# Column-first queries, values by column group and paired tables in a hybrid neighbourhood-attention and mLSTM layer

## The chip, the core and the metric

The kernel runs on one core of a Trainium2 chip. The metric is the device time of one execution in microseconds (us), and lower is better. The kernel before was run three times: 1325.43, 1327.04 and 1330.51 us, median 1327.04.

## What is computed

One layer over 2048 tokens (a grid of 32 rows by 64 columns) of width 1024. Cut to what matters:

```python
h = rmsnorm(x) * (1 + scale) + shift           # scale, shift, gate from c
proj = h @ w_in + b_in                         # 1024 -> 4624 columns
na_q, na_k, na_v, na_z, ml_q, ml_k, ml_v, ml_o, ml_z, i_f, f_f, i_b, f_b = split(proj)
# neighbourhood attention, 8 heads of 64: each query sees 8 rows x 16 columns of keys
s = (na_q * 64**-0.5) . k_neighbours + bias    # bias from rpb, outside the window -inf
na_out = softmax(s) @ v_neighbours * silu(na_z)
# bidirectional mLSTM, 4 heads of 128, chunks of 64 tokens; here a short conv goes ahead of q, k
mq, mk = silu(conv5(ml_q)), silu(conv5(ml_k))
hm = (mlstm(mq, mk, ml_v, i_f, f_f) + flipped(mlstm(...))) * sigmoid(ml_o)
ml_out = layernorm_per_head(hm) * ml_norm_w * silu(ml_z)
y = concat(na_out, ml_out) @ w_out
out = rmsnorm(x + gate * y) * final_norm_w
```

Everything is float32. A product is made of three TensorE passes over operands split into a high and a low part (`whi`, `wlo`, `hhi`, `hlo`).

## The kernel before

**Stages.** The kernel holds h for all tokens in SBUF (four groups of 512 tokens) and goes over the columns of w_in in blocks.

1. `tok_blocks` makes values token by token, one PSUM tile of 128 tokens x 256 columns after another: four blocks for the mLSTM (`vo_group`, tiles `pvo`), then two blocks, 4 and 5, for the attention values (`nav_group`, tiles `pv`). A tile is 24 matmuls; four tiles make a group of 512 tokens. VectorE adds the bias while it moves each tile into a staging tile `stv` (L581), and after the fourth tile the staging tile is stored to `d_vna` in device memory (L586). The two blocks make eight groups, so eight stores. There are two staging tiles, so group g+2 can be moved only after the store of group g has landed; and there are four PSUM tiles, so TensorE can run four tiles ahead of VectorE. Beside it a chain of small jobs runs: `decays` loads a tile `dec` of 256 KB on the SP queue (L822), POOL and ACT work on it, and the ACT queue stores it to `d_ck`; 32 such tiles go through six buffers. `tables_columns` and `tables_rows` (L670) build the tables of bias and mask in device memory, `d_t`, by copies from `d_e`, also on the SP queue.
2. `conv_blocks` makes the mLSTM's q and k with the short conv.
3. `phase1b` runs the two mLSTM passes, whose small matmuls are interleaved with a stream of large ones from `nq_gen`: the columns of mz, nz, k and q. Those for attention patches and for mz are made in patch order: TensorE writes the tile `pq` (L986), ACT moves it out with its bias (L1015, L1020), and for q and k VectorE makes the low part (L1021). At the end of each chunk of the mLSTM, `turn` transposes hm with a permutation `perm` into patch order (L1282), and `end` multiplies it into `zt` (L1288).
4. `phase2` is the attention and the output projection. A patch is 8 rows x 16 columns = 128 queries, and there are 16 patches; a unit is one patch and one pair of heads, 64 units (54 loads of a pair of tables, since a few units use the tables of an earlier one). `scores` makes the scores of both heads of two units (`pS`, L1477), VectorE adds the table `tab` and takes the minimum (L1485), ACT makes the exponential (L1486), VectorE normalises (L1497), TensorE transposes in `turned` (`pT`, L1505) and multiplies with the values (`pO`, L1520). `load_tab` (L1449) loads a table, on SP's queue, as soon as the reduce that read the same buffer is done; two units' worth of buffers exist, each of two tables. `outproj` makes `y` (L1565), adds it to x and stores the row tile to `out` (L1608, for the last patch L1599 and L1601). `load_x` (L1426), the value loads (L1405) and the stores go through POOL's queue.

**What sets the order.** Each engine works its own instructions in order, and SP's and POOL's DMA issues are such instructions. In the first stages a scheduler fixes the order when the program is built; in phase 2 it is written by hand.

The two staging tiles alternate here, and the store is held back to the middle of the next group:

```python
st = self.stage_tile(f"stv_{blk}_{g}")
for o in range(4):
    ...
    next(self.chain, None)
    if o == 1:
        self.flush()
...
self.defer(lambda: nc.sync.dma_start(dst, st[:, :, :256]))
```

Of the kernel before, what the change touches and what calls it, by code (L numbers as in the profile page):

```python
# [8 lines left out]
F32 = mybir.dt.float32  # L9
F32R = mybir.dt.float32r  # L10
AF = mybir.ActivationFunctionType
# [4 lines left out]
P = 128  # L16
# [34 lines left out]
def patch_order(ap):  # L51
    return ap.rearrange("p (r a k) -> p a r k", a=4, k=16)


def patch_ps(ap):
    return ap.rearrange("p (a r k) -> p r a k", a=4, k=16)
# [6 lines left out]
class Kernel:  # L63
# [30 lines left out]
    def scratch(self):  # L94
        d = self.dram
        self.d_vna = d.tile([T, 512], F32, name="d_vna")
# [4 lines left out]
        self.d_qna = d.tile([2, 2, 16, P, 2, P], F32, name="d_qna")  # L101
# [9 lines left out]
        self.d_t = [[d.tile([NH, P, nrs[r] * nks[t]], F32, name=f"d_t{r}{t}") for t in range(3)] for r in range(3)]  # L111
# [462 lines left out]
    def nav_group(self, blk, slot, g):  # L574
# [10 lines left out]
        dst = self.d_vna[g * GT : (g + 1) * GT, c0 : c0 + 256].rearrange("(o p) c -> p o c", p=P)  # L585
        self.defer(lambda: nc.sync.dma_start(dst, st[:, :, :256]))  # L586
# [53 lines left out]
    def tables_columns(self, ct):  # L640
# [3 lines left out]
        for i in range(16):  # L644
            c = c0 + i
            start = min(max(c - 8, 0), GRID_W - 16)
            dx = start - c + 15
            nc.sync.dma_start(self.d_e[ct][:, i, :, start - k0 : start - k0 + 16], self.d_rneg[:, :, dx : dx + 16])

    def table_fills(self):  # L650
        nc = self.nc
        for ct in range(3):
            for rt in range(3):
                t = self.d_t[rt][ct]
                n = t.shape[-1]
                dst = t.rearrange("h q k -> (h q k)").rearrange("(p j k) -> p j k", p=P, j=16)
# [3 lines left out]
    def tables_rows(self, ct, rt):  # L660
# [4 lines left out]
        for r in range(8):  # L665
# [5 lines left out]
                t[:, r * 16 : (r + 1) * 16, j0 : j0 + 8 * nk],  # L671
                self.d_e[ct][:, :, dy : dy + 8, :].rearrange("h c a k -> h c (a k)"),
# [292 lines left out]
    def nq_gen(self):  # L965
# [10 lines left out]
        for i, s, g in order:  # L976
# [35 lines left out]
            hv, lv = both[:, 0:512], both[:, 512:1024]  # L1012
            if kind in ("mz", "nz"):
                hv = hv.bitcast(F32)
                nc.scalar.activation(hv, ps, AF.Silu, bias=bias)  # L1015
# [3 lines left out]
            else:  # L1019
                nc.scalar.activation(hv, ps, AF.Identity, bias=bias)  # L1020
                nc.vector.scalar_tensor_tensor(lv, ps, bias, hv.bitcast(F32), ALU.add, ALU.subtract)  # L1021
                for e, part in enumerate((hv, lv)):
                    src = part.bitcast(F32).rearrange("p (a q) -> p a q", a=4)
                    if kind == "q":
                        dst = self.d_qna[e, ct // 2, 4 * g : 4 * g + 4, :, ct % 2].rearrange("a p q -> p a q")
# [23 lines left out]
    def phase1b(self, left, right):  # L1049
# [11 lines left out]
        self.perm = self.mle.tile([P, P], F32, name="perm")  # L1061
        nc.vector.tensor_copy(self.perm.rearrange("p (a r k) -> p a r k", r=2, k=16), patch_order(self.ident))
# [125 lines left out]
    def ml_pass2(self, ml, h):  # L1188
# [88 lines left out]
        def turn(c):  # L1277
# [4 lines left out]
            nc.tensor.transpose(ps, hm[gi][:, o, :], self.perm)  # L1282
# [533 lines left out]
```

## Time and profile before

| what | value |
|---|---|
| median of three runs | 1327.04 us |
| profiled execution, its span (the page gives no other time of it) | 1326.9 us |
| TensorE matmuls (PE) busy | 1294.6 us, 98% of the span |
| VectorE (DVE) busy | 779.6 us, 59% |
| ScalarE (ACT) busy | 542.8 us, 41% |
| GpSimd (POOL) busy | 225.1 us, 17% |
| moved by DMA | 255.91 MB, mean 193 GB/s |

The stages in time: the start and the mLSTM's values up to about 236 us, the attention's values from 236 to 329 us, the conv to about 520, the mLSTM passes with the stream of columns to about 950, the attention and output after that. A row of the views names the line, the engine, the operation and what it writes and reads; "waits" are the idle time of an engine and what ended it; PEld is TensorE's weight load, which runs beside PE; SPq, ACTq and POOLq are the queues that issue DMAs.

### The profile page before, as it was taken

What the parts mean: (1) busy time and instruction counts of PE and PEld (TensorE: products, weight loads), DVE (VectorE), ACT (ScalarE), POOL (GpSimd) and SP (SyncE); (2) the same over time, 40 slices, a digit from 0 to 9 for tenths busy, and PEclk for the clock granted to TensorE, in tenths of its full rate; (3) what the DMA queues carried; (4) which work ended last, traced back from release to release, by engine and by line L of the source; (5) the groups of instructions that cost most, each with busy time, mean ns of one, the idle gap of its engine ahead of it and who ended that gap; (6) DMA issues with size and microseconds to landing.
All of it is one profiled execution on the core that took longest, in us unless ns stands there. A gap on an engine that the chain in (4) does not pass through costs nothing. (4 is left out here: it accounts for less than half of the span.)

```text
span 1326.9 us, 23404 instructions
## 1 busy us (share of the span) xinstructions
PE 1294.6 (98%) x8330; PEld 1115.4 (84%) x8330; DVE 779.6 (59%) x2406; ACT 542.8 (41%) x1184; POOL 225.1 (17%) x280
## 2 busy tenths in 40 slices
PE   9999999999999999999999999999999999999996
PEld 8899999999878787888888888888777778778785
DVE  5754452112455559176768878767547576666663
ACT  5643324543222323123324323333356555565551
POOL 0243103331000000012212002121202211212211
PEclk9999999999999999999999999999999999999999
DMA  9998657998267685545756866746689977868871
GB/s 325 323 281 180 169 141 171 214 244 217 82 149 208 142 209 165 159 120 167 204 165 196 254 187 204 237 141 188 198 256 239 212 184 190 195 175 194 195 186 48
DMA packets 240487, 255.91 MB, mean 193 GB/s; under 512 B 31079, under 2 KB 200295, under 8 KB 240371
## 3 DMA queue, kind: packets, MB, share of 16 engines
q1 hardware_dynamic: 157006, 182.98, 50.7%
q0 software_dynamic: 20496, 36.21, 11.2%
q10 hardware_dynamic: 62868, 35.22, 9.6%
q8 instruction: 66, 1.08, 0.4%
q14 instruction: 51, 0.41, 0.1%
HBM read 169.81 MB, written 92.72 MB: 198 GB/s over the span
## 5 line engine op out<-in xcount | busy, mean ns | idle before, releaser
L986 PE MATMUL pq<-hhi,whi_a 128*128 128x512 f32 x512 | 208.2, 407 | 0.8 <-ACT u L891 0.8
L986 PE MATMUL pq<-hlo,whi_a 128*128 128x512 f32 x512 | 208.4, 407 | 0.0
L986 PE MATMUL pq<-hhi,wlo_a 128*128 128x512 f32 x512 | 206.7, 404 | 0.0
L986 PEld LDWEIGHTS pq<-hhi,whi_a 128*128 128x128 f32 x512 | 96.8, 189 | 17.8 <-ACT u L891 1.3
L986 PEld LDWEIGHTS pq<-hhi,wlo_a 128*128 128x128 f32 x512 | 96.8, 189 | 16.3
L986 PEld LDWEIGHTS pq<-hlo,whi_a 128*128 128x128 f32 x512 | 96.7, 189 | 16.0 <-issue 0.5
L1507 ACT ACTIVATE pt<-pT 96x384 f32<-96x384 f32 (+3 forms) x128 | 65.8, 514 | 86.7 <-PE pT L1505 84.0
L1486 ACT ACTIVATE pbuf<-pbuf,mn 128x480 f32<-128x480 f32 (+5 forms) x128 | 76.0, 594 | 53.0 <-DVE mn L1485 53.0
L960 POOL TENSOR_TENSOR wlo_a<-rawq,whi_a 128x1024 fp32r<-128x1024 f32 x19 | 45.8, 2409 | 296.1 <-ACT whi_a L959 263.7
L1565 PE MATMUL y<-hhi,whi_a 128*128 128x512 f32 x256 | 91.4, 419 | 0.5 <-ACT whi_a L1535 0.5
L1565 PE MATMUL y<-hhi,wlo_a 128*128 128x512 f32 (+1 forms) x272 | 90.7, 399 | 0.2 <-ACT y L1572 0.2
L1485 DVE CUSTOM_DVE_ANT_0 pbuf<-pS,tab 128x480 f32<-128x480 f32 (+5 forms) x128 | 62.9, 540 | 39.1 <-PE pS L1477 32.1
L1230 ACT ACTIVATE num<-px,gtile 128x129 f32<-128x129 f32 x120 | 38.3, 366 | 111.3 <-PE px L1225 86.5
L1505 PEld LDWEIGHTS pT<-ident,pbuf 128*128 128x128 f32 (+2 forms) x416 | 51.0, 137 | 29.6 <-issue 9.9
L618 DVE TENSOR_TENSOR stvo<-pvo,brow 128x256 f32<-128x256 f32 x64 | 26.6, 422 | 83.1 <-PE pvo L548 65.7
L1505 PE MATMUL pT<-ident,pbuf 128*128 128x128 f32 (+2 forms) x416 | 67.3, 275 | 8.2 <-DVE pbuf L1497 6.8
L546 PE MATMUL pvo<-whi_b,hhi 128*128 128x256 f32 x256 | 72.6, 284 | 0.0
L548 PE MATMUL pvo<-whi_b,hlo 128*128 128x256 f32 x256 | 72.1, 281 | 0.0
L547 PE MATMUL pvo<-wlo_b,hhi 128*128 128x256 f32 x256 | 72.0, 281 | 0.0
L1249 POOL TENSOR_TENSOR hm<-hm,ck 128x128 f32<-128x128 f32 x64 | 26.5, 414 | 252.9 <-DVE hm L1248 223.9
L833 ACT ACTIVATE dec<-dec,gtile 128x128 f32<-128x128 f32 x128 | 42.7, 393 | 53.6 <-POOL dec L826 50.8
L581 DVE TENSOR_TENSOR stv<-pv,brow 128x256 f32<-128x256 f32 x32 | 12.4, 421 | 74.4 <-DMA d_vna<-stv 43.4
(302 smaller groups left out, 3408.3 us busy)
## 6 DMA issues: line engine op xcount, KB each, us to landing
ck<-d_ck SPq DMA_DIRECT2D x64, 384.5 KB
rawq<-in_w_main_dram SPq DMA_DIRECT2D x28, 512.0 KB
raw<-in_w_main_dram SPq DMA_DIRECT2D x20, 512.0 KB
d_ck<-stvo SPq DMA_DIRECT2D x16, 514.0 KB
kv<-d_ck SPq DMA_DIRECT2D x64, 128.5 KB
wada<-in_w_ada_dram SPq DMA_DIRECT2D x32, 256.0 KB
dec<-d_mneg SPq DMA_DIRECT2D x32, 256.0 KB
d_ck<-dec ACTq DMA_DIRECT2D x32, 256.0 KB
```

Of the source, the lines that this page charges most:

```text
L546: nc.tensor.matmul(ps, lhi(k), rhi(k), start=(k == 0), stop=False)
L547: nc.tensor.matmul(ps, lhi(k), rlo(k), start=False, stop=False)
L548: self.mark = nc.tensor.matmul(ps, llo(k), rhi(k), start=False, stop=(k == KT - 1))
L833: nc.scalar.activation(t[:, o, :], t[:, o, :], AF.Exp, bias=self.cols["g"][:, d, h, c : c + 1])
L960: (eng or nc.gpsimd).tensor_tensor(lo[:, :, cs], raw, hi[:, :, cs].bitcast(F32), ALU.subtract)
L986: self.mark = nc.tensor.matmul(patch_ps(ps) if patch else ps, w, self.htok(h, g, k, patch), start=(k == 0 and n == 0), stop=(k == KT - 1 a ...
L1230: nc.scalar.activation(num[:, d, :], px[:, d, :], AF.Copy, scale=self.cols["inter"][:, d, h, c : c + 1])
L1485: nc.vector.tensor_tensor_reduce(pt[:, :nk], ps, tabs[place[u]][j][:, :nk], 1.0, 3e38, ALU.add, ALU.min, mn)
L1486: nc.scalar.activation(pt[:, :nk], pt[:, :nk], AF.Exp, bias=mn, scale=-1.0, accum_out=sums[:, j : j + 1])
L1505: nc.tensor.transpose(ps[:cs, i, :], U[u][j][:, i * cs : (i + 1) * cs], self.ident)
L1507: nc.scalar.activation(t[:cs, :nch, :], ps[:cs, :nch, :], AF.Copy)
L1565: nc.tensor.matmul(y, m[:, k, :], w[k][:, cs], start=(k == 4 and n == 0), stop=(k == 3 and n == 2))
```

## The change

A patch's 128 queries are ordered column first (column, then row) in place of row first, so loads of x and stores of the output go through 16 outer columns of 8 rows, not 8 outer rows of 16 columns. The moves that write patch order (L1015, L1020, L1021, L1288 before) therefore write with a stride of 8 floats, the transposes of hm use `ident` in place of `perm`, and one multiplication into `zt` becomes two. `d_qna` gets a layout in which a unit's q is one contiguous run of 2 KB per partition. `d_vna` becomes four tensors, one for each column group of patches (24, 32, 32 and 24 columns, which overlap); each nav group is stored by eight DMAs (two rows of the grid by four column groups) and the value load of a patch is contiguous. In the tables the heads of a pair lie side by side, `d_t` is written with 16 outer columns, and one DMA loads both tables of a unit, after the second reduce.

```diff
-        self.d_vna = d.tile([T, 512], F32, name="d_vna")
+        self.d_vna = [d.tile([ROWS, PC_NK[c], 512], F32, name=f"d_vna{c}") for c in range(4)]
...
-        self.d_qna = d.tile([2, 2, 16, P, 2, P], F32, name="d_qna")
+        self.d_qna = d.tile([2, 16, P, 2, 2, P], F32, name="d_qna")
...
+def patch_rows(ap):
+    return ap.rearrange("p (a r k) -> p a r k", a=4, k=16)
+def patch_cols(ap):
+    return ap.rearrange("p (a k r) -> p a r k", a=4, k=16)
...
-        dst = self.d_vna[g * GT : (g + 1) * GT, c0 : c0 + 256].rearrange("(o p) c -> p o c", p=P)
-        self.defer(lambda: nc.sync.dma_start(dst, st[:, :, :256]))
+        def store():
+            for c, d in enumerate(self.d_vna):
+                rows = d[8 * g : 8 * g + 8, :, c0 : c0 + 256].rearrange("(o r) c n -> r c o n", r=2)
+                for r in range(2):
+                    p0 = r * GRID_W + PC_C0[c]
+                    nc.sync.dma_start(rows[r], st[p0 : p0 + PC_NK[c], :, :256])
+        self.defer(store)
...
             nc.sync.dma_start(
-                t[:, r * 16 : (r + 1) * 16, j0 : j0 + 8 * nk],
-                self.d_e[ct][:, :, dy : dy + 8, :].rearrange("h c a k -> h c (a k)"),
+                t.rearrange("(c r) h e n -> c r (h e) n", r=8)[:, r, :, j0 : j0 + 8 * nk],
+                self.d_e[ct][:, :, dy : dy + 8, :].rearrange("h c a k -> c h (a k)"),
             )
...
+            src, hp, lp = (patch_rows(ps), patch_cols(hv), patch_cols(lv)) if patch else (ps, hv, lv)
...
-                nc.scalar.activation(hv, ps, AF.Identity, bias=bias)
-                nc.vector.scalar_tensor_tensor(lv, ps, bias, hv.bitcast(F32), ALU.add, ALU.subtract)
+                nc.scalar.activation(hp, src, AF.Identity, bias=bias)
+                if patch:
+                    for a in range(4):
+                        nc.vector.scalar_tensor_tensor(lp[:, a], src[:, a], bias, hp[:, a].bitcast(F32), ALU.add, ALU.subtract)
...
-            nc.tensor.transpose(ps, hm[gi][:, o, :], self.perm)
+            nc.tensor.transpose(ps, hm[gi][:, o, :], self.ident)
...
-            ts = slice(o * 32, (o + 1) * 32)
-            nc.vector.scalar_tensor_tensor(zt[gi][:, :, ts], ps.rearrange("p (a q) -> p a q", a=4), self.mlw[:, h : h + 1], zt[gi][:, :, ts], ALU.mult, ALU.mult)
+            for r in range(2):
+                z = zt[gi].rearrange("p a (k r) -> p a k r", r=8)[:, :, :, 2 * o + r]
+                nc.vector.scalar_tensor_tensor(z, ps.rearrange("p (r a k) -> p r a k", r=2, a=4)[:, r], self.mlw[:, h : h + 1], z, ALU.mult, ALU.mult)
...
-            src = xg[8 * pr : 8 * pr + 8, 16 * pc : 16 * pc + 16, :]
+            src = xg[8 * pr : 8 * pr + 8, 16 * pc : 16 * pc + 16, :].rearrange("r c d -> c r d")
...
-        def load_tab(u, j):
+        def load_tab(u):
...
-            (nc.gpsimd if u < 2 else nc.sync).dma_start(tabs[place[u]][j][:, :nk], self.d_t[PR_T[b // 4]][PC_T[b % 4]][2 * ct + j])
+            src = self.d_t[PR_T[b // 4]][PC_T[b % 4]][:, ct].rearrange("q e k -> q (e k)")
+            (nc.gpsimd if u < 2 else nc.sync).dma_start(tabs[place[u]][:, : 2 * nk], src)
```

**SP between the stores of two nav groups.** On the SP queue, from the store of the second group of block 4 (`stv_1`) on, stood before (each row is a line, what the DMA writes and reads, and its shape):

```order
L586 DMA d_vna<-stv_1_3013 128x4x256
L822 DMA dec_3220<-d_mneg 128x512
L207 DMA raw_0_3447<-in_w_main_dram 128x1024
L670 DMA d_t_75<-d_e_72 8x16x192
L822 DMA dec_3255<-d_mneg 128x512
L822 DMA dec_3289<-d_mneg 128x512
L822 DMA dec_3326<-d_mneg 128x512
L586 DMA d_vna<-stv_2_3153 128x4x256
```

At the same place stands now (`x2` is two of a kind; `d_vna_60` to `d_vna_63` are the four column groups):

```order
L594 DMA d_vna_60<-stv_1_3016 24x4x256 x2
L594 DMA d_vna_61<-stv_1_3016 32x4x256 x2
L594 DMA d_vna_62<-stv_1_3016 32x4x256 x2
L594 DMA d_vna_63<-stv_1_3016 24x4x256 x2
L832 DMA dec_3272<-d_mneg 128x512
L832 DMA dec_3306<-d_mneg 128x512
L832 DMA dec_3343<-d_mneg 128x512
L832 DMA dec_3377<-d_mneg 128x512
L594 DMA d_vna_60<-stv_2_3163 24x4x256 x2
```

One store has become eight, and a table copy and a load of weights no longer stand between. Counted along the queue, 19, 22, 26 and 29 of the 32 loads of `dec` stood ahead of the stores of the first four groups, and now 17, 23, 27 and 31 (two more stand between the pieces of the first store); all 32 stand ahead of the fifth in both. Of the 24 copies into the first tables, 6, 7, 8, 9 and 11 stood ahead of the first five stores, and now 15 stand ahead of each.

**SP in phase 2.** The loads of the tables of two units and the load of the next q stood so before:

```order
L1449 DMA tab_10049<-d_t_82 128x384
L1449 DMA tab_10050<-d_t_82 128x384
L1449 DMA tab_10051<-d_t_82 128x384
L1449 DMA tab_10052<-d_t_82 128x384
L1392 DMA qs_10045<-d_qna 128x2x256
```

and so now, with other table sizes at this place:

```order
L1463 DMA tab_10189<-d_t_82 128x960
L1463 DMA tab_10188<-d_t_82 128x960
```

Four issues have become two, each of twice the bytes.

**VectorE in the mLSTM passes.** The multiplication into `zt` for two chunks stood so before:

```order
L1248 SCALAR_TENSOR_TENSOR hm_1_6152<-num_6_6246,r_6_6250,hm_1_6152 128x128
L1288 SCALAR_TENSOR_TENSOR zt_0_6227<-ht_0_6269,mlw,zt_0_6227 128x4x32 x2
L1217 SCALAR_TENSOR_TENSOR ck_8_6183<-a_8_6276,ck_8_6183 128x256
```

and so now:

```order
L1261 SCALAR_TENSOR_TENSOR hm_1_6209<-num_6_6303,r_6_6307,hm_1_6209 128x128
L1302 SCALAR_TENSOR_TENSOR zt_0_6284<-ht_0_6326,mlw,zt_0_6284 128x64 x4
L1230 SCALAR_TENSOR_TENSOR ck_8_6240<-a_8_6335,ck_8_6240 128x256
```

Two instructions have become four at the same place, each over half the elements.

More of the change, by code (lines that the diff above doesn't have):

```diff
@@ L110, in scratch @@
         nrs = [11, 15, 12]
-        self.d_t = [[d.tile([NH, P, nrs[r] * nks[t]], F32, name=f"d_t{r}{t}") for t in range(3)] for r in range(3)]
+        self.d_t = [[d.tile([P, NH // 2, 2, nrs[r] * nks[t]], F32, name=f"d_t{r}{t}") for t in range(3)] for r in range(3)]
     def constants(self):
@@ L1404, in load_v @@
                     chunks[key] = p.tile([P, 512], F32, tag="v", bufs=6, name=f"v_{b}_{i}")
-                    queue.dma_start(chunks[key][: n * nkc, :], vg[r0 : r0 + n, PC_C0[pc] : PC_C0[pc] + nkc, :])
+                    queue.dma_start(chunks[key][: n * nkc, :], self.d_vna[pc][r0 : r0 + n].rearrange("r c d -> (r c) d"))
             L[b]["v"] = [
@@ L1435, in load_x @@
             L[b]["row"] = x
-        tabs = [[p.tile([P, 480], F32, name=f"tab{i}{j}") for j in range(2)] for i in range(2)]
+        tabs = [p.tile([P, 960], F32, name=f"tab{i}") for i in range(2)]
         place, follows, user = [], {}, {}
@@ L1618, in phase2 @@
             load_q(i)
-            for j in range(2):
-                load_tab(follows.pop(-1 - i), j) if j else load_tab(follows[-1 - i], j)
+            load_tab(follows.pop(-1 - i))
         self.close()
```

25 lines of the change are left out of this document (11 added, 14 removed).

## The prediction

> **What bounds the kernel now.** I read the page's busy shares and its chain first, then the waits of each stage, then single places.
>
> ```profile
> PE 1294.6 (98%) x8330; PEld 1115.4 (84%) x8330; DVE 779.6 (59%) x2406; ACT 542.8 (41%) x1184; POOL 225.1 (17%) x280
> PE 29%; DMA 4%; DVE 3%; issue 2%; ACT 1%; ACTq 0%; POOL 0%; SPq 0%; DVEq 0%; POOLq 0%
> PE y L1565 11%; PE pq L986 8%; PE pT L1505 3%; DMA tab<-d_t 3%; PE pO L1520 3%; PE pS L1477 2%; DVE pbuf L1485 1%; PE pi L1227 1%; PE px L1225 1%; DMA ck<-d_ck 0%; PE dc L1165 0%; DVE pbuf L1497 0%; PE a L1212 0%; DMA d_mix<-zt 0%; ACT hhi L1457 0%
> ```
>
> TensorE (PE) is busy for 1294.6 of 1326.9 us, so no more than 32.3 us could be gained without taking matmuls away, and the change takes none away. A gain must come from PE's few idle places, and a loss from a new one. The chain names one transfer that the change touches, the tables (`tab`), with 3%. All sums below are made against the span, 1326.9 us, the only time given of the profiled execution; it lies 0.1 us from the median of the runs, 1327.04, so no correction is made.
>
> **Part 1: the values' stores (236 to 329 us).** The waits of this stretch, then VectorE (DVE) and the SP queue in order of time (start, length, what; in brackets the idle time ahead and what ended it):
>
> ```profile
> DVE stv L581 <- DMA d_vna<-stv: 43.4, 6, 10.5
> PEld pv L546 <- DVE stv L581: 0.2, 1, 0.2
> ```
>
> ```profile
> 267.70 0.76 DVE L581 TENSOR_TENSOR stv<-pv,brow 128x256 f32<-128x256 f32 x2 [5.87 <-DMA d_vna<-stv]
> 280.07 1.09 DVE L581 TENSOR_TENSOR stv<-pv,brow 128x256 f32<-128x256 f32 x3 [6.87 <-DMA d_vna<-stv]
> 293.88 1.42 DVE L581 TENSOR_TENSOR stv<-pv,brow 128x256 f32<-128x256 f32 x4 [10.45 <-DMA d_vna<-stv]
> 304.59 1.08 DVE L581 TENSOR_TENSOR stv<-pv,brow 128x256 f32<-128x256 f32 x3 [9.30 <-DMA d_vna<-stv]
> 316.67 1.42 DVE L581 TENSOR_TENSOR stv<-pv,brow 128x256 f32<-128x256 f32 x4 [9.00 <-DMA d_vna<-stv]
> 323.21 0.43 DVE L581 TENSOR_TENSOR stv<-pv,brow 128x256 f32<-128x256 f32 x1 [1.69 <-PE pv L548]
> 326.09 0.43 DVE L581 TENSOR_TENSOR stv<-pv,brow 128x256 f32<-128x256 f32 x1 [2.45 <-PE pv L548]
> 328.97 0.43 DVE L581 TENSOR_TENSOR stv<-pv,brow 128x256 f32<-128x256 f32 x1 [2.46 <-PE pv L548]
> ```
>
> ```profile
> 263.12 0.38 SPq L586 DMA_DIRECT2D d_vna<-stv  x1
> 272.44 0.38 SPq L586 DMA_DIRECT2D d_vna<-stv  x1
> 285.43 0.40 SPq L586 DMA_DIRECT2D d_vna<-stv  x1
> 296.55 0.37 SPq L586 DMA_DIRECT2D d_vna<-stv  x1
> 309.50 0.41 SPq L586 DMA_DIRECT2D d_vna<-stv  x1
> ```
>
> DVE waited 43.4 us for the stores, and PE paid 0.2 us of it. How much was left? The last three moves are one PE tile apart, 2.88 us, so a group takes 11.5 us, and PE ended its last tile at about 328.8. Counting groups back from there, PE had its four PSUM tiles full and needed the next move at about 271.0, 282.6, 294.1, 305.7 and 317.2. The first five stores landed (the moves that waited for them began) at 267.70, 280.07, 293.88, 304.59 and 316.67, and a move itself takes 0.42. So PE's margins were 2.9, 2.1, -0.2, 0.7 and 0.1 us. A delay of the third, fourth or fifth landing is a delay of PE almost to its full length; it is lost once, since everything behind moves with it.
>
> How long is the delay? A group's eight pieces hold 112 columns for each 64, since the column groups overlap: 512 KB becomes 896 KB, 0.393 MB more. What the DMAs move here, and how full they are (share, then GB/s, last two columns):
>
> ```profile
> 260.00:280.00 20.00, 20.00 (x172) 20.00 (x171) 4.29 (x7) 7.93 (x23) 8.32 (x7) 1.00 0.95 208
> 280.00:300.00 20.00, 20.00 (x168) 19.79 (x168) 2.93 (x8) 9.28 (x28) 8.22 (x7) 1.00 1.08 247
> 300.00:320.00 20.00, 20.00 (x170) 20.00 (x169) 5.26 (x10) 7.93 (x22) 5.15 (x4) 1.00 0.85 223
> ```
>
> With a share of 0.85 to 1.08 they are as good as full, at a mean of 226 GB/s. At that rate a group's extra bytes take 1.74 us, and five groups' 8.7 us by the fifth landing. The order adds to it: of the table copies, 15 now stand ahead of the fifth store, not 11.
>
> ```profile
> 392.83 19.17 SPq L670 DMA_DIRECT2D d_t<-d_e  x24
> ```
>
> 24 such copies took 19.17 us, 0.8 us each, so four more are 3.2 us. All 32 loads of `dec` stand ahead of the fifth store in both orders, so they add nothing at that point. Together 11.9 us, against a margin of 0.1: **+12 us**. Eight issues of 0.37 to 0.41 us last 3 us where one lasted 0.4, but they are issued while the transfers queue, so I add nothing for them. The gain's end: PE waits 0.2 us here, so no more than 0.2 can be won. The loss's end: 14.6 us at the fourth store (three groups' bytes 5.2, two more `dec`, and six more table copies 4.8; a `dec` is loaded and stored, 0.52 MB, 2.3 us each), and 2.6 us for the seven added issues of 0.37 if nothing hides them: +17. I take +12, near the upper end, because the margins are near nothing and the DMAs near full; the lower end, 0, is kept for the case that transfers fit into the last few per cent or that the waiting `dec` jobs are what fills the queue. SP's work behind the waiting stores is the loads of the next weights and the remaining table copies for the conv; PE idles there a few us in all, and I give the conv 0, with ends -2 and +2.
>
> **Part 2: the strided moves in the mLSTM passes (520 to 1000 us).** DVE's groups that change (count, busy, mean ns), a row of windows, and PE's waits:
>
> ```profile
> L1288 DVE SCALAR_TENSOR_TENSOR zt<-ht,mlw,zt 128x128 f32<-128x128 f32 x60 | 18.8, 344 | 2.6 <-DMA zt<-d_zml 1.3 <-issue 0.9 <-PE ht L1282 0.3
> L1021 DVE SCALAR_TENSOR_TENSOR qst<-pq,bcol,qst 128x512 fp32r<-128x512 f32 x16 | 11.9, 745 | 3.1 <-ACT qst L1020 3.1
> 755.00:850.00 95.00, 92.69 (x517) 79.00 (x516) 75.78 (x284) 32.33 (x79) 16.16 (x20) 1.00 0.69 204
> PE ht L1282 <- ACT hm L1274: 1.5, 2, 1.2
> PE px L1225 <- DVE st L1149: 1.4, 2, 0.7
> ```
>
> From 344 ns for 128 elements and 745 for 512, one element costs 1.04 ns and an instruction 210. Each of 64 multiplications into `zt` becomes two of 64 elements: 64 x 210 ns = 13.4 us more. Each of 16 moves of q's low part becomes four of 128 elements: 4 x 344 - 745 = 631 ns, 10.1 us more. DVE gets 23.5 us more over 480 us, in which it was busy 75 to 80% (75.78 of 95 in the window shown). PE waited for DVE 1.4 us and for ACT 1.5 us over that stage, so half a per cent of DVE's work reached PE; the stream of large matmuls covers the rest. Five times that share of 23.5 us is 0.6 us. I take **+1**, with ends 0 and +5; if the stream ran dry, all of the 23.5 us would be in PE's way.
>
> What does the stride itself cost? The nearest row moves 16 elements with a stride of 64 bytes:
>
> ```profile
> L620 DVE TENSOR_TENSOR gates<-pvo,bgate x16: 173/175/178, 48.7 to 130.8; 128x16 f32<-128x16 f32 x16
> L1337 DVE TENSOR_TENSOR nwt<-rstd x48: 151/161/166, 605.5 to 942.3; 128x4 f32<-128x4 f32 x48
> ```
>
> Against 161 ns for 4 contiguous elements, 12 more at 1.04 ns give 173.5, and 175 was measured: no cost of the stride is seen, over few elements and on DVE alone. The Trainium skill speaks against this change here: "SBUF — State Buffer", in the note on SBUF "cachelines", says that each access that crosses to a new line of 16 bytes pays a penalty, so that fp32 strides freely only up to 4 elements, and the new stride is 8. The row above does not agree with it; for ACT no row shows a strided write. What a slow stride would make of the time is a rival below.
>
> **Part 3: the tables (950 to 1320 us).** DVE's and PE's waits in this stage, and PE's idle places that they end in:
>
> ```profile
> DVE pbuf L1485 <- DMA tab<-d_t: 6.8, 8, 1.6
> PE pT L1505 <- DVE pbuf L1497: 6.8, 6, 2.0
> 1055.27 0.52 PE L1505 MATMUL pT<-ident,pbuf 128*128 128x128 f32 x3 [1.59 <-DVE pbuf L1497]
> 1150.54 0.52 PE L1505 MATMUL pT<-ident,pbuf 128*128 128x128 f32 x3 [2.01 <-DVE pbuf L1497]
> 1233.61 0.50 PE L1505 MATMUL pT<-ident,pbuf 128*96 128x128 f32 x3 [0.55 <-DVE pbuf L1497]
> 1253.79 0.52 PE L1505 MATMUL pT<-ident,pbuf 128*120 128x128 f32 x3 [0.59 <-DVE pbuf L1497]
> ```
>
> ```profile
> 1053.63 0.53 DVE L1485 CUSTOM_DVE_ANT_0 pbuf<-pS,tab 128x352 f32<-128x352 f32 x1 [1.62 <-DMA tab<-d_t]
> 1042.64 10.86 DMA tab<-d_t
> ```
>
> Four of the six PE waits follow a late table; they sum to 4.7 us. The table behind the first was 10.86 us under way and 1.62 us late. With pairs the first table of a unit is asked for one reduce later (0.53 us), but SP issues one DMA where it issued two, and x, q and values cross more DMA engines beside it, so the last piece should come earlier. To take away a wait, 1.6 us of 10.9 must go, 15%. I take **-4**, with ends -4.7 and, if the later issue decides, 8 waits longer by 0.53, +4.2. With the table in time, the next that is late is ACT's exponential, off PE's path. The loads of q, values and x wait for nothing that PE shows, so their faster transfers count nothing.
>
> **Part 4: the end.**
>
> ```profile
> 1320.51 0.65 SPq L1601 DMA_DIRECT2D out_dram<-xr  x1
> 1320.74 0.69 ACTq L1599 DMA_DIRECT2D out_dram<-xr  x1
> ```
>
> The span ends at 1326.9, 5.5 us after the last issue, its length included. Each of the two stores holds 256 KB in 8 outer rows, now 16 outer columns. If half of the 5.5 us is transfer, and it halves, 1.4 is gained: **-1.5**, ends 0 and -2.7.
>
> Sum: 1326.9 + 12 + 1 - 4 - 1.5 = 1334.4 us.
>
> **The rivals.**
> - *The stores stay hidden.* The third to fifth landing need only keep within 0.1 to 0.7 us. For it: the first store's pieces stand behind 17 to 19 `dec` loads, not 19, and DVE's 9 to 10 us waits say that a store's own transfer (4.6 us for the first: 263.12 to 267.70) was a small part and its place in the queue the larger. Against it: more bytes into full DMAs. It decides if the delay at the fifth landing stays under 0.5 us. Time: 1326.9 - 4 - 1.5 = 1321.4. This is the case on the other side, not slower.
> - *The stores are late by part of it*, because the table copies fill gaps that now stand empty: +6, less 4 and 1.5, plus 0.5: 1327.9.
> - *The stride is slow on ACT or DVE.* If every strided move doubles, DVE gets 64 x 2 x 277 ns and 16 x 4 x 344 ns (57 us; 277 for 64 elements by the slope above) on top of the 23.5 of part 2. In the window shown it has 19 of 95 us free, some 95 over the stage, so it would be busy nearly throughout, and PE would wait for `px` and `ht`: I put a sixth of the 57 us in PE's way, +10. Time: 1344. By the rule of the Trainium skill named in part 2, this is the one that comes.
> - *The tables are no faster*: -4 becomes 0 or more, 1338; it lies in the range of the forecast.
>
> **How the numbers follow.** The forecast has 0.42 (1330 to 1343, by parts 1 and 3), hidden stores 0.28, part of it 0.18, slow strides 0.12. The predicted time is the forecast's, 1334.5. About 0.5% or 6.6 us is what a measurement of this kernel can tell from no change: 1320.4 and 1333.7 are the limits. Of the hidden case 0.6 lies below 1320.4: faster 0.17. Of the forecast 0.6 lies above 1333.7, and slow strides do: slower 0.37. The rest, 0.46, is the same; cases of both signs hold much of the chance, and the forecast alone would have 1330 to 1343. The range reaches down into the hidden case, 1319, and up to 1344.
>
> **What would show it.** In the profile after: PE waits for `stv` between 260 and 330 us of some 12 us, and the mLSTM's passes begin that much later (right), or none (hidden); the strided `zt` rows near 277 ns, the ACT moves near 680 (or doubled); no `pT` wait behind `tab`; under 5.5 us behind the last issue. The forecast is wrong if PE's waits in the nav stretch stay under 3 us, or if a stage not named here moves by over 3 us.

## The result and the profile after

The changed kernel took 1348.09 us (median of 4 runs, 1344.76 to 1351.34), the kernel before 1328.34 (4 runs): the ratio is 1.0144, 95% interval [1.0110, 1.0178]. That is slower by 1.4%; forecast were 1334.5 us and a range to 1344.

The page of the kernel after, busy shares and the chain's lines:

```profile
PE 1298.7 (97%) x8330; PEld 1118.2 (83%) x8330; DVE 802.3 (60%) x2517; ACT 566.5 (42%) x1184; POOL 216.9 (16%) x278
PE pq L996 18%; PE y L1579 13%; PE pc L550 4%; PE pc L551 4%; PE pc L552 4%; PE pO L1534 3%; PE pT L1519 3%; PE pvo L611 3%; PE pS L1491 3%; DMA dec<-d_mneg 2%; DMA d_ck<-dec 2%; PE pvo L550 2%; PE pvo L551 2%; PE pvo L552 2%; PE pi L1240 2%
```

PE does the same 8330 matmuls and is idle for 46.5 us of 1345.2, not 32.3 of 1326.9; DVE has 22.7 and ACT 23.7 us more to do. The tables have left the chain. It now holds `dec` too, but that is no comparison: the chain of the kernel before was followed over some 40% of the span only, from about 810 us on, and does not reach the stretch of `dec`. The time of the profiled run is listed as 1347.27 us for a span of 1345.2: some 2 us of a run lie outside the span, which the prediction had put at nothing.

The first and last PE instructions of the tiles cut the span into stages (us; "nav" is the attention's values, from the first `pv` to the first `pc`; the mLSTM goes from the first `pq` to the first `pS`; the end is what lies behind the last `y` began):

| kernel | up to first `pv` | nav | conv | mLSTM | phase 2 | end | span |
|---|---|---|---|---|---|---|---|
| before | 237.4 | 91.4 | 190.9 | 439.7 | 357.1 | 10.4 | 1326.9 |
| after | 242.7 | 101.9 | 190.1 | 448.0 | 350.7 | 11.8 | 1345.2 |
| difference | +5.3 | +10.5 | -0.8 | +8.3 | -6.4 | +1.4 | +18.3 |

The first stage, which the prediction did not name, moved by more than the 3 us that it had given as a sign of being wrong.

**Up to the first `pv`.** The waits of the kernel after from 100 to 240 us, and its window from 170 to 190 us (PE busy, PEld, DVE, ACT, POOL, then granted clock, DMA share, GB/s):

```profile
DVE gsum L519 <- DMA ga<-in_w_ada_dram: 9.1, 6, 4.5
PE ps_c_w L723 <- DVE gtile L813: 3.7, 1, 3.7
```

```profile
170.00:190.00 20.00, 16.25 (x128) 16.08 (x127) 9.31 (x21) 2.93 (x5) 0.19 (x2) 0.93 0.55 142
```

DVE waited for `ga`, weights of the gate; behind that wait in DVE's order stood the copy to `gtile` that PE needs. Neither wait was there before. PE stood for 3.75 us at L723, and a granted clock of 0.93 over these 20 us, where it had been 1.00, makes some 1.4 us more (an estimate, 0.07 of 20). `ga` is loaded by SP, between the copies `d_e<-d_rneg` that build the columns of the tables. The edit turns these copies round as well, from 8x15x16 to 15x8x16 elements, which the section on the change leaves out. They, before and after:

```profile
L648 SPq DMA_DIRECT2D d_e<-d_rneg x48: 608/609/1157, 142.7 to 200.5; - x48
```

```profile
L658 SPq DMA_DIRECT2D d_e<-d_rneg x48: 779/780/1399, 142.4 to 195.9; - x48
```

An issue now takes 0.78 us and not 0.61, and the copies end sooner all the same: more of them stand ahead of each load of `ga`, 46 ahead of its last pair where 31 had stood. That pair was issued at 193 us, before at 180.

**Nav.** Waits, and SP's issues of the stores, of the kernel after:

```profile
DVE stv L585 <- DMA d_vna<-stv: 34.1, 3, 14.7
PE pv L550 <- DVE stv L585: 8.7, 3, 4.5
```

```profile
275.18 10.63 SPq L594 DMA_DIRECT2D d_vna<-stv  x8
291.09 9.16 SPq L594 DMA_DIRECT2D d_vna<-stv  x8
304.28 11.80 SPq L594 DMA_DIRECT2D d_vna<-stv  x8
```

PE waits 8.7 us for DVE where it waited 0.2, and the granted clock was 0.98 over the stretch, some 2 us of its 101.9 (before 1.00); together that is about the 10.5. Eight issues take 9 to 12 us of SP's time, not the 3 us that eight times 0.38 would be.

**mLSTM.** ACT's moves in the kernel before, then the moves in patch order and PE's waits of that stage in the kernel after:

```profile
L1015 ACT ACTIVATE qst<-pq,bcol x32: 669/688/691, 525.7 to 939.6; 128x512 f32<-128x512 f32 x32
```

```profile
L1026 ACT ACTIVATE qst<-pq,bcol x32: 1195/1266/1309, 540.7 to 961.5; 128x512 f32<-128x512 f32 x32
L1034 DVE SCALAR_TENSOR_TENSOR qst<-pq,bcol,qst x64: 407/464/507, 780.7 to 1022.5; 128x128 fp32r<-128x128 f32 x64
L1302 DVE SCALAR_TENSOR_TENSOR zt<-ht,mlw,zt x120: 304/334/369, 631.3 to 960.6; 128x64 f32<-128x64 f32 x120
```

```profile
PE ht L1295 <- ACT hm L1287: 3.7, 3, 1.9
PE pi L1240 <- DVE num L1245: 1.7, 1, 1.7
```

ACT's moves went from 688 to 1266 ns at the median, DVE's parts take 464 ns for 128 elements and 334 for 64, where 344 and 277 had been worked out.

**Phase 2.** No wait for `tab` is left. The transfers on POOL's queue (KB, median us to landing) before, then after:

```profile
xr<-in_x_dram POOLq DMA_DIRECT2D x15, 512.0 KB, 8.9
out_dram<-xr POOLq DMA_DIRECT2D x15, 512.0 KB, 7.2
v<-d_vna POOLq DMA_DIRECT2D x16, 256.0 KB, 9.1
```

```profile
xr<-in_x_dram POOLq DMA_DIRECT2D x15, 512.0 KB, 5.0
out_dram<-xr POOLq DMA_DIRECT2D x15, 512.0 KB, 3.7
v<-d_vna POOLq DMA_DIRECT2D x16, 256.0 KB, 6.0
```

So these transfers land sooner, as the change meant; what it pays for lies elsewhere.

**The end.** The transfer of the last row tile is faster too: from the issue on ACT's queue to the landing that SP waits for it took 5.15 us before and 3.37 now. But the trace lists a last instruction `DRAIN` on POOL, which took 9.59 us, from 1334.82 to 1344.41; the closing steps of all engines come behind it, 3.3 us after the last store landed at 1341.08. Before, this drain took 1.83 us and was over before the store was issued.

### The profile page after: what moved, and what is told of

Its sections match the earlier page's. It is cut to its first block, busy times and chain, and to the rows that moved or that the text cites. A ratio compares the mean times of both kernels' runs of the same rounds, so it can differ in the third digit from the quotient of the medians.

```text
span 1345.2 us, 23440 instructions
## 1 busy us (share of the span) xinstructions
PE 1298.7 (97%) x8330; PEld 1118.2 (83%) x8330; DVE 802.3 (60%) x2517; ACT 566.5 (42%) x1184; POOL 216.9 (16%) x278
## 4 chain that ended last, share of the span: by engine, by line
PE 73%; DMA 8%; DVE 7%; ACT 4%; issue 3%; SPq 1%; POOL 1%; ACTq 0%; POOLq 0%; DVEq 0%
PE pq L996 18%; PE y L1579 13%; PE pc L550 4%; PE pc L551 4%; PE pc L552 4%; PE pO L1534 3%; PE pT L1519 3%; PE pvo L611 3%; PE pS L1491 3%; DMA dec<-d_mneg 2%; DMA d_ck<-dec 2%; PE pvo L550 2%; PE pvo L551 2%; PE pvo L552 2%; PE pi L1240 2%
## 5 line engine op out<-in xcount | busy, mean ns | idle before, releaser
L996 PEld LDWEIGHTS pq<-hlo,whi_a 128*128 128x128 f32 x512 | 96.8, 189 | 15.9 <-issue 0.5
L1519 PEld LDWEIGHTS pT<-ident,pbuf 128*128 128x128 f32 (+2 forms) x416 | 50.8, 136 | 23.7 <-ACT pt L1521 5.2
L585 DVE TENSOR_TENSOR stv<-pv,brow 128x256 f32<-128x256 f32 x32 | 12.6, 421 | 84.9 <-DMA d_vna<-stv 34.1
```

What stands on the lines that cost most here:

```text
L996: self.mark = nc.tensor.matmul(patch_ps(ps) if patch else ps, w, self.htok(h, g, k, patch), start=(k == 0 and n == 0), stop=(k == KT - 1 a ...
L1519: nc.tensor.transpose(ps[:cs, i, :], U[u][j][:, i * cs : (i + 1) * cs], self.ident)
```

## The experiments

Theory: four places, each with its own cause, as in the table of stages. Each kernel below undoes or isolates one. The kernels of the first group ran on one chip, with the kernel before at 1331.60 us; those of the second on another, before at 1327.12; those of the third with before at 1330.53, and the last run with before at 1329.54. In the second group each was run once, so there the profile is what counts.

### The copies of columns

```diff
# against after
-...self.d_e[ct][:, i, :, start - k0 : start - k0 + 16].rearrange("h a k -> a h k"), self.d_rneg[:, :, dx : dx + 16].rearrange("h a k -> a h k"))
+...self.d_e[ct][:, i, :, start - k0 : start - k0 + 16], self.d_rneg[:, :, dx : dx + 16])
```

> The changed kernel, with only the copies d_e<-d_rneg in the old shape (8x15x16, not 15x8x16). After the change 48 of them took 780 ns each on SP where they had taken 608, the loads of ga behind them came up to 13 us later, and PE waited 3.7 us at L723 for gtile. If the copies' length is the cause: 608 ns again, no wait at L723, the first pv matmul some 5 us earlier (237 to 239 us, not 242.7), about 5 us off the whole. Rival, the order in which the scheduler put the copies is the cause and not their length: the wait at L723 stays above 2 us and the time within 1 us of the changed kernel. In both, the eight stores per group still cost PE about 9 us and ACT's moves still take 1.2 us.

Measured: 1347.87 us, 1.0123 of before [1.0108, 1.0138]. The copies take 609 ns, no wait at L723 is left, and the first `pv` came at 237.7 us, 4.9 to 7.0 earlier than in the other kernels of its group. So the turned copies are the cause of the 5.3 us. Whether by the length of their issue or by their order the run can't tell: with the old shape the scheduler's old order came back too (31 copies ahead of the last pair of `ga`, as before the change), so the rival of the expectation stays open. Of what was gained, nav took back a part: it was 109.1 us long, the longest of all, against 106.9 and 107.6 in the two kernels of this group with the same stores. The 5 us expected off the whole don't show; the changed kernel itself did not run on this chip, and the stage is the measure.

### One store per group

```diff
# against after
-        self.d_vna = [d.tile([ROWS, PC_NK[c], 512], F32, name=f"d_vna{c}") for c in range(4)]
+        self.d_vna = d.tile([T, 512], F32, name="d_vna")
...
-                    nc.sync.dma_start(rows[r], st[p0 : p0 + PC_NK[c], :, :256])
+        self.defer(lambda: nc.sync.dma_start(dst, st[:, :, :256]))
```

> The changed kernel, with values kept in one tensor in token order: one store of 512 KB per nav group, and value loads as before. If the eight stores (their bytes or their number) are the cause of PE's 8.7 us of waits for stv: those waits fall under 1 us and the nav stretch (first pv to first pc matmul) goes from 101.9 to 91.5 us, some 10 us off the whole. Rival, the copies of tables and loads of dec moved in the queue are the cause: the wait stays at 5 us or more. Value loads in phase 2 go back to about 9 us to landing; if they mattered there, phase 2 (first pS to last y) grows from 350.7 by over 1 us.

Measured: 1339.36 us, 1.0061 [1.0042, 1.0080]; it is the only one of the group clearly nearer to before. Nav was 96.3 us, PE's waits 3.5, where 91.5 and under 1 were expected: most of the nav loss is gone, and 3 to 5 us stay. Phase 2 took 353.9 us here and 352.1 when the same kernel was run again, beside 352.1 of the changed one on that chip: the faster value loads (6.0 us, here 9.1) are worth nothing that these runs show.

### The side on which the stride lies

```diff
# against after
-            src, hp, lp = (patch_rows(ps), patch_cols(hv), patch_cols(lv)) if patch else (ps, hv, lv)
+            src, hp, lp = (patch_read(ps), patch_write(hv), patch_write(lv)) if patch else (ps, hv, lv)
+def patch_read(ap):
+    return ap.rearrange("p (a r k) -> p a k r", a=4, k=16)
+def patch_write(ap):
+    return ap.rearrange("p (a k r) -> p a k r", a=4, k=16)
```

> The changed kernel, with the moves of pq that make patch order reading PSUM with a stride of 16 floats and writing SBUF one float after another, in place of reading runs of 16 and writing with a stride of 8. The result in memory is the same. If the strided write is what made ACT's 48 moves of q, z and mz 1.25 us long where they had been 0.69: they fall below 0.9 us, and the mLSTM stage (first pq to first pS) goes from 448 to about 442 us. If any access of single floats is slow, on PSUM's side too, they stay at 1.2 us or more and the time is the same within 2 us.

Measured: ACT's moves, and DVE's, of this kernel:

```profile
L1034 ACT ACTIVATE qst<-pq,bcol x32: 668/688/692, 549.1 to 965.8; 128x512 f32<-128x512 f32 x32
L1042 DVE SCALAR_TENSOR_TENSOR qst<-pq,bcol,qst x64: 311/341/351, 787.5 to 1024.9; 128x128 fp32r<-128x128 f32 x64
```

They are back at 688 and at the worked-out 344. So on ACT it is the write of single floats to SBUF at a stride of 8 that costs, 1.1 ns an element ((1266 - 688) / 512). On DVE the strided access to SBUF costs 1.0 ((464 - 341) / 128); there the high part `hp` was also read from SBUF with the stride, and the run doesn't part the read from the write. The read of single floats from PSUM at a stride of 16 costs nothing. The Trainium skill, "SBUF — State Buffer", says in its note on SBUF "cachelines" that a line of 16 bytes needs at least two hits for full bandwidth, and that each access that crosses to a new line pays. The trace agrees with that for these accesses, one float in each 32 bytes; what two floats do, the last run below shows. The mLSTM stage fell by 4.1 us to 443.9, and it fell in each kernel with these moves: it took 446.4 to 449.8 us in the eight kernels with the strided write, 442.2 to 443.9 in the three with the strided read, and 439.2 to 441.2 in the three with the old order. The whole, 1347.08 us, was not below its group: its nav took 106.9 us.

### The old order of queries

```diff
# against after
-            src, hp, lp = (patch_rows(ps), patch_cols(hv), patch_cols(lv)) if patch else (ps, hv, lv)
+            src, hp, lp = ps, hv, lv
...
-            nc.tensor.transpose(ps, hm[gi][:, o, :], self.ident)
+            nc.tensor.transpose(ps, hm[gi][:, o, :], self.perm)
...
-            src = xg[8 * pr : 8 * pr + 8, 16 * pc : 16 * pc + 16, :].rearrange("r c d -> c r d")
+            src = xg[8 * pr : 8 * pr + 8, 16 * pc : 16 * pc + 16, :]
```

> The changed kernel, with a patch's queries in the old order, row first: moves of pq and products into zt as before the change, x and output in 8 outer rows. Values, tables in pairs and q's layout stay as changed. If the column-first order is the cause of what the mLSTM stage lost: first pq to first pS goes from 448 back to 440 us and ACT's moves to 0.69 us, with 16 fewer us in ACT and DVE at their places, 8 us off the whole. The end behind the last y matmul tells whether the output in 16 columns is the cause of 11.8 us there where 10.4 had been: 10.4 again if so. If x and output over 16 columns had sped up phase 2, it grows from 350.7 us by over 1 us; if the tables alone did it, it stays.

Measured: 1346.46 us, 1.0115 [1.0099, 1.0130]. The mLSTM stage is 439.2 us, as before the change: the column-first order costs there 8.8 us, of which the strided access makes 4.1 by the run above. That the rest is DVE's added instructions is not shown by this run; the last one tests it. x and output are slow again (8.3 and 6.9 us to landing), DVE waits 10.3 us for `tab`, and phase 2 is 352.8 us; the changed kernel took 350.7 and, run again, 352.1, so the growth is 0.7 to 2.1 us and leaves the question of the expectation open. The end is 10.7 us, and POOL's last drain took 2.57.

### Bytes or pieces

One store per group is the measure; the second kernel cuts it into eight pieces of 64 KB, the third stores 384 KB more in a second DMA to memory that nobody reads. The changed kernel ran beside them.

> The changed kernel once more, on the same chip as the three runs with it, to see how much its nav stretch varies: it took 101.9 us in the first profile (PE waiting 8.7 us for stv), and two kernels with the same stores took 106.9 and 107.6 us on another chip. If it is the chip's DMA that decides, it lies within 2 us of 107 here; if it varies from run to run, anywhere between 100 and 109.

> One store of 512 KB per nav group, else as changed; the measure for the two runs below. It took 96.3 us in the nav stretch, PE waiting 3.5 us; within 2 us of that again.

```diff
# against one store
-        self.defer(lambda: nc.sync.dma_start(dst, st[:, :, :256]))
+        def store():
+            for p0 in range(0, P, 16):
+                nc.sync.dma_start(dst[p0 : p0 + 16], st[p0 : p0 + 16, :, :256])
+        self.defer(store)
```

> As one store per group, but the store is cut into eight DMAs of 16 partitions, 64 KB each, with no byte more than 512 KB. If the number of DMAs is the cause (each issue on SP waits for an earlier one, so that eight take 9 to 12 us and hold up the loads of dec behind them): the nav stretch is over 100 us, near that of the changed kernel, and eight issues take over 6 us. If the added bytes are the cause: within 2 us of the kernel with one store.

```diff
# against one store
-        self.defer(lambda: nc.sync.dma_start(dst, st[:, :, :256]))
+        def store():
+            nc.sync.dma_start(dst, st[:, :, :256])
+            nc.sync.dma_start(self.d_spare[g, blk - 4], st[0:96, :, :256])
+        self.defer(store)
```

> As one store per group, and a second DMA stores 96 of the 128 partitions once more to memory that nobody reads: 896 KB per group in two DMAs, the bytes of the changed kernel. If the bytes are the cause (0.393 MB at 226 GB/s, 1.7 us for each of five groups): the nav stretch is some 8 us longer than with one store, near that of the changed kernel. If the number of DMAs is the cause: within 2 us of the kernel with one store.

Measured (the `dec` loads and table copies are those ahead of the fifth store in SP's order):

| kernel | DMAs, KB per group | `dec`, copies ahead | nav us | PE's wait for `stv` us |
|---|---|---|---|---|
| before (first profile) | 1, 512 | 32, 11 | 91.4 | 0.0 (PEld 0.2) |
| one store again | 1, 512 | 32, 25 | 94.1 | 2.9 |
| eight pieces | 8, 512 | 32, 15 | 102.1 | 8.7 |
| more bytes | 2, 896 | 32, 23 | 102.0 | 7.3 |
| after again | 8, 896 | 32, 15 | 106.2 | 11.2 |

Neither theory alone holds: the pieces cost 8.0 us without a byte more, the bytes cost 7.9 without more pieces, and both together 12.1. Each of the two is twice the 4 us by which the changed kernel itself varies (101.9 us in its first profile, 106.2 here). That both together cost less than the sum of the two, 15.9, lies within these 4 us, with one profile of each, and is not shown. The copies ahead are not the price: one store has 25 and is the fastest of the four. The eight issues, here those of one group in the kernel with eight pieces:

```profile
297.16 8.07 SPq L593 DMA_DIRECT2D d_vna<-stv  x8
```

and the one of a group in the kernel with one store:

```profile
291.79 0.37 SPq L590 DMA_DIRECT2D d_vna<-stv  x1
```

SP is held for 8 us at 64 KB a piece. The trace names the semaphore of each DMA: those of SP and ACT take turns on eight, and seven of the eight pieces shown wait for their own, that is for the DMA that used it last. Over 255 to 350 us the pieces waited 23.7 us for the stores `d_ck<-dec` of ACT's queue, in 7 places; the single stores waited 5.8, in 2. That this wait is the price of the pieces is argued, not shown; the next run bears on it.

### The stores on another queue

```diff
# against after
-                    nc.sync.dma_start(rows[r], st[p0 : p0 + PC_NK[c], :, :256])
+                    nc.gpsimd.dma_start(rows[r], st[p0 : p0 + PC_NK[c], :, :256])
```

> The changed kernel with the 64 stores of values issued on POOL's queue, not SP's. Same bytes, same pieces, SP's loads of dec no longer behind them. If the eight issues held up SP (9 to 12 us for eight on it, 4 loads of dec behind): the nav stretch falls from 106.2 to about 102, what the bytes alone cost. If the transfers themselves, being many, are the cost: it stays at 105 or more; POOL's mask work on dec then stands behind the issues, which could make it longer still.

Measured: 1347.70 us, 1.0125 [1.0103, 1.0147], nav 104.1 us with 8.8 us of PE's waits. That lies between the two outcomes and within what the changed kernel varies by (101.9 and 106.2). Whether the hold of SP or the many transfers is what the pieces cost stays open.

### The tables alone, and a kernel with the costs out

```diff
# against before
-            (nc.gpsimd if u < 2 else nc.sync).dma_start(tabs[place[u]][j][:, :nk], self.d_t[PR_T[b // 4]][PC_T[b % 4]][2 * ct + j])
+            src = self.d_t[PR_T[b // 4]][PC_T[b % 4]][:, ct].rearrange("q e k -> q (e k)")
+            (nc.gpsimd if u < 2 else nc.sync).dma_start(tabs[place[u]][:, : 2 * nk], src)
```

> The kernel before with the tables in pairs alone (and the copies d_t<-d_e and q's layout that go with them): queries row first, one store per nav group, copies d_e<-d_rneg as before. If the pairs are what shortened phase 2 (357.1 us before, 350.7 to 353.9 in the kernels with pairs): 351 to 354 us there, no pT matmul waiting behind a late table, mLSTM stage 440 and the first pv at 237, so the whole is some 4 us faster than before, ratio 0.996 to 0.998. The order of table copies (21 ahead of the fifth nav store, 11 before) may cost up to 3 us in the nav stretch, 91.4 before. If faster x, output and values were what shortened phase 2, it stays at 356 or 357 and the ratio at 1.0.

Measured: 1325.48 us, 0.9967 [0.9951, 0.9984]. Phase 2 took 353.4 us. Its waits there:

```profile
DVE pbuf L1491 <- DMA tab<-d_t: 6.6, 4, 2.4
PE pT L1511 <- DVE pbuf L1503: 4.9, 4, 1.9
```

DVE still waits 6.6 us for tables, in 4 places and not 8; PE 4.9 and not 6.8. So with the pairs phase 2 is 3.7 us shorter, as expected, but DVE's wait for `tab` hardly falls; in all kernels with x and output over 16 columns it was 3.2 us or less, in the two with pairs and row-first order 6.6 and 10.3. Phase 2 itself is 352.8 and 353.4 us in these two and 350.2 to 354.1 in the others with pairs: what faster x and output add lies within that spread.

As much as in phase 2 was gained in a stage that the expectation doesn't name. The conv took 186.8 us, 4.1 less than before. Two of the waits of the kernel before in that stretch:

```profile
PE kt L939 <- ACT acc_k L930: 3.7, 3, 2.1
ACT stk L941 <- DMA d_ck<-stk: 29.0, 9, 7.4
```

With the pairs alone, PE's wait is gone there and ACT's is 5.4 us. More of the 72 table copies lie ahead of the conv, and fewer beside it: the conv took 186.3 to 188.2 us in the seven kernels that left 33 to 42 copies to it, and 188.8 to 192.8 in the seven that left 56 to 61. No run changed this order alone, so the copies as the cause are likely and not shown.

The mended kernel is the changed one with the edits of the first three experiments together (old column copies, one store, stride on the read).

> The changed kernel with its three costs taken out: values in one tensor with one store per group, copies d_e<-d_rneg in the old shape, and moves of pq that read PSUM with the stride and write in order. Kept: column-first queries with x and output over 16 columns, tables in pairs, products into zt in two. Expected by stage: first pv at 237.5 (242.7 changed), nav 92 to 96, mLSTM stage 443 to 444, phase 2 350 to 353, end 9 to 12: 1326 to 1330 us with before at 1328, ratio 0.997 to 1.003. If the costs aren't separate (what one gives back another takes), it stays over 1.005. Against the run with the pairs alone it tells what the column-first order is worth net of DVE's added products.

Measured: 1323.42 us, 0.9945 [0.9928, 0.9961], faster than before by 0.55%, and 2.0% below the changed kernel by the two ratios. It came out faster than expected (0.997 at best). By stage: 238.3, nav 96.1, conv 186.8, mLSTM 443.3, phase 2 350.4, end 8.9. Against the one profile of the kernel before, the span is 3.1 us shorter (the runs on this chip put the gain at 7.1): nav, mLSTM and the first stage lose 9.2 us, and phase 2 gives 6.7, the conv 4.1 and the end 1.5. So a large part of the gain is the conv's, which the expectation had not counted. The kernel with the pairs alone, in the same group, is 2.1 us slower, with an interval that overlaps this one; that is what the column-first order is worth on top of the pairs, and it is not clear of the noise. Its transfers:

```profile
xr<-in_x_dram POOLq DMA_DIRECT2D x15, 512.0 KB, 5.4
out_dram<-xr POOLq DMA_DIRECT2D x15, 512.0 KB, 3.7
```

### One product in place of two

```diff
# against the mended kernel
-            for r in range(2):
-                z = zt[gi].rearrange("p a (k r) -> p a k r", r=8)[:, :, :, 2 * o + r]
-                nc.vector.scalar_tensor_tensor(z, ps.rearrange("p (r a k) -> p r a k", r=2, a=4)[:, r], self.mlw[:, h : h + 1], z, ALU.mult, ALU.mult)
+            z = zt[gi].rearrange("p a (k r) -> p (a k) r", r=8)[:, :, 2 * o : 2 * o + 2]
+            nc.vector.scalar_tensor_tensor(z, ps.rearrange("p (r q) -> p q r", r=2), self.mlw[:, h : h + 1], z, ALU.mult, ALU.mult)
```

> The mended kernel, with the product into zt of a chunk in one instruction of 128x64x2 (pairs of floats, one pair in each 8) in place of two of 128x64. In the mended kernel the mLSTM stage took 443.3 us, 3.6 more than before the change, and the 128 products of 339 ns are the larger part of what DVE does there beyond it. If that is the cause: the one instruction takes 340 to 400 ns, some 18 to 20 us leave DVE, the stage goes to 440 to 442 us, and the whole is 1 to 3 us faster than the mended kernel (0.9945 of before): 0.992 to 0.994. If the instruction takes 650 ns or more, strides cost DVE what was saved, and if the stage stays over 443 with short products, the rest comes from q's moves in four pieces.

Measured: 1324.24 us, 0.9946 [0.9926, 0.9967], no faster than the mended kernel. The product, of this kernel:

```profile
L1303 DVE SCALAR_TENSOR_TENSOR zt<-ht,mlw,zt x60: 331/346/361, 613.9 to 937.3; 128x128 f32<-128x128 f32 x60
```

346 ns for 64 pairs of floats, each pair 32 bytes from the next, is as short as the 344 of the old product in runs of 32. So two floats in each 32 bytes cost nothing where one cost 1 ns. DVE's work in the stage fell by 12 us (18 to 20 were expected) and the stage by 1.1 to 442.2, of the 3.6 by which the mended kernel lay over the kernel before. So the added products are not shown to be the larger part of that. Phase 2 was 354.1 us in that profile, 3.7 more than in the mended kernel, for which the change gives no reason, and the whole showed no gain.

## Why the prediction was wrong

- **Part 1, the stores: right in size, wrong in part of the why.** Forecast +12, measured +10.5, and 106.9 to 109.1 us (+15.5 to +17.7) in the runs of the first group. PE's margins of 0.1 to 0.7 us and the bytes held: bytes alone cost 7.9, as the 8.7 worked out for them. The step "they are issued while the transfers queue, so I add nothing for them" failed: eight pieces of the same bytes cost 8.0 us. The +3.2 for table copies failed the other way: with one store, 25 copies stood ahead of the fifth store and nav was 94.1 us, in the kernel before 11 and 91.4, and with eight pieces 15 and 102.1. A term too high stood in for one put at nothing, and that the sum of +12 came near is in part luck.
- **A term that was not in the sum: +5.3.** Part 1 looked at where the copies `d_t<-d_e` stand, and never at the copies `d_e<-d_rneg` that the same edit turns round. It saw only the nav stretch of SP's order. Their issue went from 0.61 to 0.78 us, and more of them got ahead of `ga`; PE stood for 3.75 us behind it. This term stood at nothing without a reason.
- **Part 2, the strided moves: +1 forecast, +8.3 measured; this step failed most.** The step took the stride for free, from a row of 16 elements (175 ns against 173.5 worked out), and judged it on DVE alone though ACT had 48 of the moves. ACT's rose by 0.58 us each, DVE's by 0.06 to 0.12. With that, the rival of slow strides came true in its mechanism, on ACT above all: ACT's busy time in the stage rose by 23 us and DVE's by 21, and the stage lost 8.3 where the rival had put 1 + 10. The rule of the Trainium skill that spoke against the change ("SBUF — State Buffer", the note named in part 2) was the better witness. The row of 16 elements could not have decided it: at 1 ns an element the stride would make 16 ns there, and the comparison was with another instruction that reads no PSUM, while the prediction's own numbers put the fixed part of an instruction at 210 ns in one row and at 157 (161 less 4 elements) in the other.
- **Part 3, the tables: -4 forecast, -6.4 measured.** The size is right for the pairs: alone, they took phase 2 from 357.1 us to 353.4, and to 352.8 in the kernel with the old order. The path is right in part: PE's wait behind `pbuf` fell from 6.8 to 4.9 us, but DVE still waited 6.6 and 10.3 us there for `tab`, 6.8 before, so the tables alone did not come in time. With x and output over 16 columns beside them the wait is 3.2 us or less; part 3 had named this as a help. What it adds to the stage, 3 us at most, is within the spread of the kernels. The kernel before has one profile only.
- **Part 4, the end: -1.5 forecast, +1.4 measured.** The transfer is faster as thought, 3.37 us from the last issue and not 5.15. The step that failed is that the span ends with the transfer: POOL's last drain, 1.83 us before, took 9.59 in the four kernels with column-first order and stores in eight pieces to four tensors on SP, and there it ends last (11.7 to 11.8 us). In the six column-first kernels with values in one tensor it took 5.02 and in the one with POOL's stores 6.08; there the transfer ends last again, and the end is 8.8 to 8.9 us, so -1.5 was reached. What POOL drains for so long the trace doesn't say.
- **The base.** The span was taken for the run; the 2 us outside it would have moved the forecast up by as much.

The signed sum shows it: +12 +1 -4 -1.5 = +7.5 was forecast, and +5.3 +10.5 -0.8 +8.3 -6.4 +1.4 = +18.3 measured. The sign and the largest term were right. Two terms, the copies' 5.3 and the 7.3 by which part 2 fell short, make 12.6 us; the other differences take 1.8 of it back, which leaves the 10.8 that the sum was short. The measured time, 1348.09 us, lies above the range, which ended at 1344.

## What to carry to other kernels

A transfer that lands sooner is worth only what waits for it; count ahead of that what the new layout asks of the engines that write it. Go through every DMA that an edit touches, and price its issue and what is queued behind it: the ones not looked at cost 5.3 us here. Put a reordering on the side of the access that is free (here the read from PSUM, or pairs of floats) and measure it with an instruction of the same length on the same engine. And where the margin is under 1 us, as at these stores, neither more bytes nor more pieces are free: change a layout where DMA and queue have room.

## What the runs showed of the hardware

- A write of single floats to SBUF 32 bytes apart costs 1.1 ns an element more on ACT (1266 ns against 688 for 512), and an instruction of DVE that reads and writes SBUF in this way 1.0 (464 against 341 for 128); pairs of floats 32 bytes apart cost nothing (346 ns against 344), nor does a read of single floats from PSUM 64 bytes apart (688 ns as before).
- A stop of PE costs more than itself: in the window from 170 to 190 us of the kernel after, where PE stood for 3.75 us, the granted clock was 0.93, against 1.00 before, and the stage lost 5.3 us.
- Turning a copy of 8x15x16 elements into 15x8x16 lengthened its issue on SP from 0.61 to 0.78 us.
- POOL's last drain took 1.67 to 2.57 us in the three row-first kernels and 5.02 to 9.59 in the column-first ones; at 9.59 it ended 3.3 us after the last store had landed.
